# Two-layer hybrid decoder on one core: two idle token corners lent to the weight loads, adding evictions of 512 columns, and a new table of places for the wide products

## The chip, the cores and the metric

The kernel runs on 1 core of one Trainium2 chip. The metric is device microseconds of one execution; the time of a kernel is the median of several timed runs. Engines are named as in the profile: PE (TensorE), PEld (its weight loads), DVE (VectorE), ACT (ScalarE), POOL (GpSimd), SP (SyncE, here only an issuer of DMAs).

## What is computed

A causal decoder trunk of two layers over 256 tokens of width 2048, in float32:

```
for i in range(2):
    h = rms_norm(x, mix_norm_g[i])
    x = x + (fox_attention(h) if i == 0 else dilated_attention(h))
    h = rms_norm(x, mlp_norm_g[i])
    a = relu(h @ mlp_w_up[i])            # 2048 -> 8192
    x = x + (a * a) @ mlp_w_down[i]      # 8192 -> 2048
```

Layer 0 mixes with 16 heads of softmax attention with a cumulative forget-gate bias, layer 1 with three groups of dilated windows. For this change the two MLPs matter: each reads 64 MiB of `mlp_w_up` and 64 MiB of `mlp_w_down` once.

## The kernel before

**Products in three matmuls.** A weight tile is 256 rows by 512 columns (`raw`, 512 KB, two row chunks of 128). It is loaded by a DMA that SP issues (L386), cast on ACT to a rounded high part `wh` (L411), and DVE subtracts to get the low part `wl` (L412). Activations are held in the same two parts, with tokens along the stationary side. Each 128x128 by 128x512 product is three matmuls: high by high, high by low, low by high (L457 to L459). One such weight tile, used for two row chunks and two halves of the 256 tokens, is twelve matmuls; it is called a plain unit below, and the kernel counts such units (`woven["count"]`).

**The MLP in blocks.** An MLP is worked in four blocks b of 2048 inner columns: the up products of block b in four column chunks n, squared relu, and the down products of block b, whose sums are added into the residual `x`. Between them the inner activations are turned around by way of memory: DVE transposes (`turned`, L1088), POOL issues the DMAs that write `held` (L1082), SP issues the DMA that reads `back` (L367), and ACT and DVE split `back` into `aTh` (L1113) and `aTl` (L1117, L1120).

**Wide pieces.** Block 0's up products are plain units. The up products of blocks 1 to 3 are done in six wide pieces, two column chunks each, by a scheme with seven products where the plain way has eight. A piece is 8 triples and 4 single units. A triple takes two `raw` tiles (loaded crosswise) and makes three units: the first of `raw` itself, the second of differences `sd` (L408), the third of `v` (L414, L415). On DVE a triple is the op on `sd`, two of half size for `v`, and three for `wl`; on PE it is three units of six matmuls each (L1167 to L1169), into six PSUM banks. A single unit is one more `raw` tile for six matmuls. When a piece is complete, DVE combines the six banks in six ops (`c`, L1134 to L1141), ACT does relu and square (L1146, L1153, L1076), and the way around memory follows.

**Order.** All engines are fed in the order in which the program is traced; `pin` ties every engine to it. The wide units are woven between plain units by the table `WIDE_AT`: row i holds, for piece i, the counts of plain units behind which its 8 triples and its 4 single units stand (the third unit of a triple stands one count later). Counts 0 to 63 are block 0 (up, then down), 64 to 95 the down products of block 1, 96 to 127 of block 2, 128 to 159 of block 3. In blocks 2 and 3 three of the four down products are done in two halves.

**Buffers.** There are 5 `raw` tiles, 5 `wh` and 5 `wl`. When unit u has been traced on PE, the split (cast and subtract) of unit u+5 is traced behind it, and then the loads for which a `raw` tile comes free. So a split can start when PE has done the unit five places back, and DVE can be ahead of PE by up to five units. SP's loads each wait for the split that frees their tile, and SP works strictly in order: a `back` move that waits for its `held` writes holds up the loads behind it.

**Late evictions.** The down products of blocks 0 to 2, and the first halves of block 3's, are added into `x` by DMA (`late`): ACT scales the PSUM bank into a buffer `y` (L1020) and POOL issues a DMA that adds it to `x` (L1021). For each product there are four such evictions of 256 columns; the two of token half 0 use the two `bias` buffers, those of half 1 the buffers `t0` and `t2`. The next product uses the same two PSUM banks, so its first matmul waits for these evictions; the token halves are ordered so that half 0 is complete six matmuls before half 1.

**Tokens.** The normalised tokens are held as eight tiles `hT` (L566), each two chunks of 128 columns, high and low part, 256 tokens. In the wide scheme the second chunk of a pair with the second token half (the corner) is read by none of the seven products, only by block 0's plain up products.

Of the kernel before, what the change touches and what calls it, by code (L numbers as in the profile page):

```python
# [9 lines left out]
F32 = mybir.dt.float32  # L10
# [3 lines left out]
ALU = mybir.AluOpType  # L14
# [35 lines left out]
WIDE_AT = ((15, 19, 23, 27, 30, 32, 33, 34, 37, 38, 39, 39),  # L50
# [79 lines left out]
def trunk(ctx: ExitStack, tc, x, fox_w_in, fox_b_f, fox_q_gain, fox_k_gain, fox_w_out, dil_w_in,  # L130
# [244 lines left out]
    state = {"raw": 0, "split": 0, "done": 0}  # L375
    raws, splits = [], []

    def load():
# [3 lines left out]
        t = wpool.tile([P, RAW_SUB, NC], F32, tag="raw", name=f"raw{i}", bufs=RAW_BUFS)  # L382
# [67 lines left out]
    def product_steps(acc, keys, lhs, steps, post=None, begin=0, end=KC - 1):  # L450

        def three(k, t):
            hi, lo = (in_turn(w[:, k % W_SUB, :]) for w in splits[used[0]])
            ah, al = lhs(k)
            tok = slice(t * P, (t + 1) * P)
            first, last = k == begin, k == end
            nc.tensor.matmul(acc[t], ah[:, tok], hi, start=first, stop=False)  # L457
            nc.tensor.matmul(acc[t], ah[:, tok], lo, start=False, stop=False)  # L458
            nc.tensor.matmul(acc[t], al[:, tok], hi, start=False, stop=last)  # L459
# [45 lines left out]
    def last_product(keys, lhs, ready, begin):  # L505
# [7 lines left out]
        for k, x in steps:  # L513
# [4 lines left out]
            ah, al = lhs(k)  # L518
            tok = slice(t * P, (t + 1) * P)
            first, last = k == begin, k == KC - 1  # L520
            to = acc[x][:, 0:cols.stop - cols.start]
            nc.tensor.matmul(to, ah[:, tok], hi, start=first, stop=False)
            nc.tensor.matmul(to, ah[:, tok], lo, start=False, stop=False)
            nc.tensor.matmul(to, al[:, tok], hi, start=False, stop=last)
# [11 lines left out]
    def norm_begin(tag):  # L536
        rstd[tag] = small.tile([P, NT], F32, tag="rstd", name=f"rstd_{tag}", bufs=2)
        hT[tag] = [None] * (KC // 2)
        return small.tile([P, NT, NX], F32, tag="ssp", name=f"ssp_{tag}", bufs=2)

    def transposed_by_dma(tag, col, n):
# [22 lines left out]
        for half in range(2):  # L564
            pr = n * 2 + half
            both = act.tile([P, 2, 2, S], F32R, tag="hT", name=f"hT_{tag}_{pr}", bufs=KC // 2)  # L566
            if tag != "n2":
# [8 lines left out]
                of = [(both[:, i, 1, :], room[i].rearrange("p t n -> p (t n)"), both[:, i, 0, :]) for i in range(2)]  # L576
                for _, whole, hi in of:
                    nc.scalar.copy(hi, whole)
# [769 lines left out]
```

## Time and profile before

| | before |
|---|---|
| median of 3 timed runs | 2090.97 us (2090.74 to 2092.85) |
| profiled execution, its own time | 2093.61 us |
| its span | 2091.9 us |
| granted TensorE clock, mean | 0.999 |
| busy: PE, DVE, ACT, POOL | 2074.1, 1782.8, 1336.6, 319.8 us |
| HBM read and written | 488.29 MB, 40.39 MB |

The profile is of one execution. A row of the timeline gives start, duration, engine, line, operation and, in brackets, how long the engine stood idle before it and what ended that. Consecutive like instructions are merged (x4). A row of a list of waits gives who waited for whom, the total in us, the number of times and the longest. A row of a list of groups gives count, busy time, mean ns of one and the idle time before them. Matmuls are pipelined: a 512-column matmul is shown as 0.38 us long, while the next starts some 0.216 us after it.

### The profile page before, as it was taken

The page shows a single profiled execution, that of the slowest core. Times are in us where ns is not written, and L with a number is a line of the kernel's source. Part 1 is how long each engine was busy: PE and PEld are TensorE (multiplying, and loading weights), DVE is VectorE, ACT ScalarE, POOL GpSimd, SP SyncE. Part 2 cuts the span into 40 slices and gives each one's busy share as a digit, 9 for nine tenths or more (in the row PEclk, how much of TensorE's full clock was granted, in tenths as well). Part 3 has the DMA queues.
Part 4 walks back from the last instruction along what each step waited for, and adds up shares of the span by engine and source line. Part 5 has one row for each costly group of instructions (what it writes and reads, how often), then busy time and mean ns, then how long its engine had stood idle before and what let it go on. Part 6 is the DMA issues. An engine that isn't in the chain of part 4 may idle for free.

```text
span 2091.9 us, 29264 instructions
## 1 busy us (share of the span) xinstructions
PE 2074.1 (99%) x9791; PEld 1809.8 (87%) x9791; DVE 1782.8 (85%) x2267; ACT 1336.6 (64%) x1889; POOL 319.8 (15%) x446
## 2 busy tenths in 40 slices
PE   9999999999999999999999999999999999999999
PEld 7888888888888888888888888888888888888888
DVE  6788876899999999997768787767999998999985
ACT  6665654867676676775656565646767666667663
POOL 2000000113120213312010010000113031132240
PEclk9999999999999999999999999999999999999999
DMA  8888887888898999989977776867888898899896
GB/s 258 255 259 262 259 247 216 267 278 284 263 304 250 282 278 282 302 264 285 283 241 230 248 243 210 267 205 239 270 272 284 269 291 261 280 274 283 281 289 195
DMA packets 366295, 549.55 MB, mean 263 GB/s; under 512 B 44648, under 2 KB 151488, under 8 KB 366144
## 3 DMA queue, kind: packets, MB, share of 16 engines
q1 hardware_dynamic: 336800, 511.61, 76.4%
q0 software_dynamic: 28928, 35.68, 8.0%
q8 instruction: 77, 1.26, 0.2%
q14 instruction: 74, 0.61, 0.1%
q10 hardware_dynamic: 416, 0.39, 0.1%
HBM read 488.29 MB, written 40.39 MB: 253 GB/s over the span
## 4 chain that ended last, share of the span: by engine, by line
PE 76%; DVE 11%; DMA 6%; issue 4%; ACT 2%; POOL 0%; SPq 0%; DVEq 0%; ACTq 0%
PE acc L457 20%; PE acc L458 20%; PE acc L459 20%; DVE wl L412 7%; DMA raw<-in_mlp_w_up_dram 3%; DMA raw<-in_mlp_w_down_dram 2%; DVE sd L408 2%; PE wide_n_tp L1169 2%; PE wide_n_tp L1168 2%; PE wide_n_tp L1167 2%; PE wide_n_sc L1168 1%; PE wide_n_sc L1169 1%; PE wide_n_sc L1167 1%; PE wide_n_acc L1169 1%; PE wide_n_acc L1168 1%
## 5 line engine op out<-in xcount | busy, mean ns | idle before, releaser
L412 DVE TENSOR_TENSOR wl<-raw,wh 128x1024 fp32r<-128x1024 f32 (+1 forms) x755 | 910.7, 1213 | 240.9 <-ACT wh L411 232.2
L411 ACT CAST wh<-raw 128x1024 fp32r<-128x1024 f32 (+1 forms) x755 | 782.1, 1044 | 467.3 <-PE acc L459 307.1
L457 PE MATMUL acc<-wh,hT_n 128*128 128x512 f32 x1152 | 437.9, 380 | 0.2 <-ACT hT_n L653 0.2
L458 PE MATMUL acc<-wl,hT_n 128*128 128x512 f32 x1152 | 437.0, 379 | 0.5 <-DVE wl L412 0.5
L459 PE MATMUL acc<-wh,hT_n 128*128 128x512 f32 x1152 | 436.8, 379 | 0.0
L459 PEld LDWEIGHTS acc<-wh,hT_n 128*128 128x128 f32 x1152 | 217.7, 189 | 31.4 <-DVE hT_n L654 0.4
L458 PEld LDWEIGHTS acc<-wl,hT_n 128*128 128x128 f32 x1152 | 217.9, 189 | 30.8 <-DVE wl L412 1.8
L457 PEld LDWEIGHTS acc<-wh,hT_n 128*128 128x128 f32 x1152 | 217.9, 189 | 30.1 <-ACT hT_n L653 0.4
L1021 POOL DMA_DIRECT2D x<-y_n x144 | 128.8, 1242 | 524.2 <-ACT y_n L1020 522.5
L457 PE MATMUL acc<-wh,aTh_n1a 128*128 128x512 f32 x512 | 194.6, 380 | 3.7 <-ACT y_n L1020 3.7
L458 PE MATMUL acc<-wl,aTh_n1a 128*128 128x512 f32 x512 | 194.2, 379 | 0.1
L459 PE MATMUL acc<-wh,aTl_n1a 128*128 128x512 f32 x512 | 194.0, 379 | 0.0
L457 PE MATMUL acc<-wh,aTh_n3a 128*128 128x512 f32 x480 | 183.1, 382 | 3.3 <-ACT y_n L1020 3.2
L458 PE MATMUL acc<-wl,aTh_n3a 128*128 128x512 f32 x480 | 182.9, 381 | 0.2 <-DVE wl L412 0.2
L459 PE MATMUL acc<-wh,aTl_n3a 128*128 128x512 f32 x480 | 182.5, 380 | 0.0
L411 ACT CAST wh<-sd 128x1024 fp32r<-128x1024 f32 x96 | 100.7, 1049 | 116.8 <-DVE sd L408 110.7
L408 DVE TENSOR_TENSOR sd<-raw,raw 128x1024 f32<-128x1024 f32 x96 | 116.9, 1218 | 8.5 <-DMA raw<-in_mlp_w_up_dram 7.4
L411 ACT CAST wh<-v 128x1024 fp32r<-128x1024 f32 x96 | 100.9, 1051 | 36.2 <-PE acc L459 17.9
L412 DVE TENSOR_TENSOR wl<-v,wh 128x1024 fp32r<-128x1024 f32 x96 | 116.7, 1216 | 3.5 <-ACT wh L411 3.2
L412 DVE TENSOR_TENSOR wl<-sd,wh 128x1024 fp32r<-128x1024 f32 x96 | 116.6, 1215 | 0.5 <-ACT wh L411 0.4
L457 PEld LDWEIGHTS acc<-wh,aTh_n1a 128*128 128x128 f32 x512 | 96.8, 189 | 19.3 <-ACT y_n L1020 5.7
L458 PEld LDWEIGHTS acc<-wl,aTh_n1a 128*128 128x128 f32 x512 | 96.8, 189 | 14.2 <-DVE wl L412 0.6
(667 smaller groups left out, 3465.3 us busy)
## 6 DMA issues: line engine op xcount, KB each, us to landing
raw<-in_mlp_w_up_dram SPq DMA_DIRECT2D x304, 512.0 KB, 4.9
raw<-in_mlp_w_down_dram SPq DMA_DIRECT2D x256, 512.0 KB, 5.3
raw<-in_dil_w_in_dram SPq DMA_DIRECT2D x192, 256.0 KB, 3.5
raw<-in_fox_w_in_dram SPq DMA_DIRECT2D x94, 512.0 KB, 4.9
x<-y_n POOLq DMA_DIRECT2D x144, 128.0 KB, 6.6
raw<-in_fox_w_out_dram SPq DMA_DIRECT2D x32, 512.0 KB, 5.0
raw<-in_dil_w_in_dram SPq DMA_DIRECT2D x32, 512.0 KB, 4.7
raw<-in_dil_w_out_dram SPq DMA_DIRECT2D x32, 512.0 KB, 3.7
```

The costliest lines, as they stand in the source:

```text
L408: nc.vector.tensor_sub(quarters[0], raw, raws[n - 1][:, 1, :].unsqueeze(1).to_broadcast([P, RAW_SUB, NC]))
L411: nc.scalar.copy(hi[:, part, :], raw[:, part, :])
L412: nc.vector.tensor_sub(lo[:, part, :], raw[:, part, :], hi[:, part, :].bitcast(F32))
L457: nc.tensor.matmul(acc[t], ah[:, tok], hi, start=first, stop=False)
L458: nc.tensor.matmul(acc[t], ah[:, tok], lo, start=False, stop=False)
L459: nc.tensor.matmul(acc[t], al[:, tok], hi, start=False, stop=last)
L1021: nc.gpsimd.dma_start(xt[n][:, t, h * HC:h * HC + HC], y, accum_op=ALU.add)
L1167: nc.tensor.matmul(banks[bank], ah, wh, start=what < 3 and of == 0, stop=False, **alone)
L1168: nc.tensor.matmul(banks[bank], ah, wl, start=False, stop=False, **alone)
L1169: nc.tensor.matmul(banks[bank], al, wh, start=False, stop=of == KC // 2 - 1, **alone)
```

## The change

1. **Tokens in three tiles.** Each norm now puts its tokens into one large tile `hT` and two smaller ones with tag `hc`, reached by `tokens_of`. For the MLP norms (n1, n3) the two `hc` tiles hold the corners, four pairs each; for n0 and n2 they hold the last two pairs. In the MLP norms the second chunk of a pair is now split in two ops of 128 columns on ACT and two on DVE, where one of 256 stood.
2. **Two more raw tiles.** An `hc` tile is as large as a `raw` tile. From the end of block 0's up products until the down products of block 3 begin (`corners["free"]`), loads may go into the two `hc` tiles too, so that 7 weight tiles are loaded or held instead of 5. Each of the two sets is refilled as its oldest tile is used up.
3. **Adding evictions of 512 columns.** Per token half one eviction and one adding DMA of 512 columns, both halves in the `bias` buffers, instead of two of 256.
4. **The table `WIDE_AT`**: most triples and single units stand 1 or 2 counts earlier.
5. Side effects of 1: the gate product of layer 0 reads high and low parts interleaved; its small tiles share one tile `gates`.

```
 WIDE_AT = ((16, 19, 23, 27, 30, 32, 33, 35, 37, 38, 39, 39),      # was 15, 19, 23, 27, 30, 32, 33, 34, 37, 38, 39, 39
            (41, 43, 45, 47, 49, 51, 53, 56, 58, 58, 58, 60),      # was 42, 44, 47, 49, 51, 52, 55, 56, 58, 58, 60, 61
...
            (117, 119, 120, 122, 124, 126, 127, 129, 131, 131, 131, 131))  # was 118, 120, 122, 123, 125, 126, 127, 128, 131, 131, 132, 132
...
+    pooled, corners = [0], {"free": False, "users": []}
...
-        t = wpool.tile([P, RAW_SUB, NC], F32, tag="raw", name=f"raw{i}", bufs=RAW_BUFS)
+        if corners["free"] and len(corners["users"]) < 2:
+            t = act.tile([P, RAW_SUB, NC], F32, tag="hc", name=f"raw{i}", bufs=2)
+            corners["users"].append(i)
+        else:
+            t = wpool.tile([P, RAW_SUB, NC], F32, tag="raw", name=f"raw{i}", bufs=RAW_BUFS)
+            pooled.append(i)
...
-        while state["done"] in spent:
-            state["done"] += 1
-        while state["raw"] < min(len(plan), state["done"] + RAW_BUFS):
+        while state["raw"] < len(plan):
+            for users in (pooled, corners["users"]):
+                while users and users[0] in spent:
+                    users.pop(0)
+            if len(pooled) >= RAW_BUFS and not (corners["free"] and len(corners["users"]) < 2):
+                break
             load()
...
-                of = [(both[:, i, 1, :], room[i].rearrange("p t n -> p (t n)"), both[:, i, 0, :]) for i in range(2)]
+                of = [(tokens(pr, 0, 1), room[0], tokens(pr, 0, 0))]
+                of += [(tokens(pr, 1, 1, t), room[1][:, t], tokens(pr, 1, 0, t)) for t in range(NT)]
...
+            hT[tag].append(act.tile([P, KC // 2 * 6 * P], F32R, tag="hT", name=f"hT_{tag}"))
+            hT[tag] += [act.tile([P, 8 * P], F32R, tag="hc", name=f"hc_{tag}_{n}", bufs=2) for n in range(2)]
...
             if late:
-                for h in range(2):
-                    of, bufs = ("bias", 2) if t == 0 else (("t0", "t2")[h], 1)
-                    y = work.tile([P, HC], F32, tag=of, name=f"y_{scale}_{n}_{t}_{h}_{used[0]}", bufs=bufs)
-                    nc.scalar.activation(y, by_column(acc[t])[:, 0, h, :], AF.Copy, scale=rstd[scale, 2][:, t:t + 1])
-                    nc.gpsimd.dma_start(xt[n][:, t, h * HC:h * HC + HC], y, accum_op=ALU.add)
+                y = work.tile([P, NC], F32, tag="bias", name=f"y_{scale}_{n}_{t}_{used[0]}", bufs=2)
+                nc.scalar.activation(halves(y), by_column(acc[t]), AF.Copy, scale=rstd[scale, 2][:, t:t + 1])
+                nc.gpsimd.dma_start(xt[n][:, t, :], y, accum_op=ALU.add)
...
+            corners["free"] = b < 3
```

How the table moves instructions is shown at two places of the first MLP. The first is on DVE, at the last two triples of its last wide piece (in the table's last row, counts 127 and 128 before, 127 and 129 now). A triple is the row that writes `sd`, the row for `wl` from `raw` behind it, two rows for `v`, and the rows for `wl` from `sd` and from `v`; a row for `wl` from `raw` elsewhere is a plain unit. Before:

```order
1017 L412 TENSOR_TENSOR wl_8917<-raw_8827,wh_8916 128x1024
1018 L412 TENSOR_TENSOR wl_8935<-v_8890,wh_8934 128x1024
1019 L408 TENSOR_TENSOR sd_8946<-raw_8860,raw_8829 128x1024
1020 L412 TENSOR_TENSOR wl_8945<-raw_8860,wh_8944 128x1024
1021 L414 TENSOR_TENSOR v_8947<-raw_8860,sd_8946 128x512
1022 L415 TENSOR_TENSOR v_8947<-raw_8829,v_8947 128x512
1023 L412 TENSOR_TENSOR wl_8964<-sd_8946,wh_8963 128x1024
1024 L412 TENSOR_TENSOR wl_8974<-raw_8896,wh_8973 128x1024
1025 L412 TENSOR_TENSOR wl_9004<-v_8947,wh_9003 128x1024
1026 L408 TENSOR_TENSOR sd_9015<-raw_8920,raw_8898 128x1024
1027 L412 TENSOR_TENSOR wl_9014<-raw_8920,wh_9013 128x1024
```

The same place of DVE now:

```order
1027 L418 TENSOR_TENSOR wl_8837<-raw_8702,wh_8836 128x1024
1028 L418 TENSOR_TENSOR wl_8849<-v_8798,wh_8848 128x1024
1029 L414 TENSOR_TENSOR sd_8866<-raw_8726,raw_8724 128x1024
1030 L418 TENSOR_TENSOR wl_8865<-raw_8726,wh_8864 128x1024
1031 L420 TENSOR_TENSOR v_8867<-raw_8726,sd_8866 128x512
1032 L421 TENSOR_TENSOR v_8867<-raw_8724,v_8867 128x512
1033 L418 TENSOR_TENSOR wl_8884<-sd_8866,wh_8883 128x1024
1034 L418 TENSOR_TENSOR wl_8894<-raw_8759,wh_8893 128x1024
1035 L418 TENSOR_TENSOR wl_8918<-v_8867,wh_8917 128x1024
1036 L418 TENSOR_TENSOR wl_8928<-raw_8787,wh_8927 128x1024
1037 L414 TENSOR_TENSOR sd_8941<-raw_8806,raw_8804 128x1024
1038 L418 TENSOR_TENSOR wl_8940<-raw_8806,wh_8939 128x1024
```

Between one triple and the next there was one plain unit (1024); now there are two (1034, 1036).

The second place is on ACT, at the end of block 0's last down product, where its sums are evicted and block 1 begins (`c` are tiles of the wide piece that has just been completed). Before:

```order
541 L411 CAST wh_6063<-raw_5979 128x1024
542 L1113 CAST aTh_n1a_0_6054<-back_n1a_0_1_5965 128x4x128
543 L1153 ACTIVATE c_n1a_2_3_6086<-wide_n_1_2_tp_5303 128x512
544 L411 CAST wh_6088<-sd_6065 128x1024
545 L1146 ACTIVATE c_n1a_2_1_5915<-c_n1a_2_1_5915 128x512
546 L1076 ACTIVATE c_n1a_2_3_6086<-c_n1a_2_3_6086 128x512
547 L1076 ACTIVATE c_n1a_2_1_5915<-c_n1a_2_1_5915 128x512
548 L411 CAST wh_6110<-raw_6002 128x1024
549 L1020 ACTIVATE y_n_3_0_0_247_6122<-acc_0_5832,rstd_n_4109 128x256
550 L1020 ACTIVATE y_n_3_0_1_247_6125<-acc_0_5832,rstd_n_4109 128x256
551 L1020 ACTIVATE y_n_3_1_0_247_6137<-acc_1_5833,rstd_n_4109 128x256
552 L1020 ACTIVATE y_n_3_1_1_247_6140<-acc_1_5833,rstd_n_4109 128x256
```

Now:

```order
545 L417 CAST wh_6042<-raw_5930 128x1024
546 L1133 CAST aTh_n1a_0_6055<-back_n1a_0_0_5932 128x4x128
547 L1166 ACTIVATE c_n1a_2_1_5901<-c_n1a_2_1_5901 128x512
548 L1133 CAST aTh_n1a_0_6055<-back_n1a_0_1_5948 128x4x128
549 L1096 ACTIVATE c_n1a_2_3_6040<-c_n1a_2_3_6040 128x512
550 L1096 ACTIVATE c_n1a_2_1_5901<-c_n1a_2_1_5901 128x512
551 L417 CAST wh_6077<-sd_6044 128x1024
552 L417 CAST wh_6099<-raw_5946 128x1024
553 L1040 ACTIVATE y_n_3_0_247_6118<-acc_0_5828,rstd_n_4109 128x512
554 L1040 ACTIVATE y_n_3_1_247_6131<-acc_1_5829,rstd_n_4109 128x512
```

Two evictions stand where four stood, and the relu (L1153 before) has moved ahead of these rows; the casts, the squares and one more cast of `back` still stand between the first cast and the evictions.

More of the change, by code (lines that the diff above doesn't have):

```diff
@@ L453, in three @@
             hi, lo = (in_turn(w[:, k % W_SUB, :]) for w in splits[used[0]])
-            ah, al = lhs(k)
-            tok = slice(t * P, (t + 1) * P)
+            ah, al = (x[t] for x in lhs(k))
             first, last = k == begin, k == end
-            nc.tensor.matmul(acc[t], ah[:, tok], hi, start=first, stop=False)
-            nc.tensor.matmul(acc[t], ah[:, tok], lo, start=False, stop=False)
-            nc.tensor.matmul(acc[t], al[:, tok], hi, start=False, stop=last)
+            nc.tensor.matmul(acc[t], ah, hi, start=first, stop=False)
+            nc.tensor.matmul(acc[t], ah, lo, start=False, stop=False)
+            nc.tensor.matmul(acc[t], al, hi, start=False, stop=last)
         for k in steps[::W_SUB]:
@@ L565, in transposed_by_dma @@
             pr = n * 2 + half
-            both = act.tile([P, 2, 2, S], F32R, tag="hT", name=f"hT_{tag}_{pr}", bufs=KC // 2)
+            tokens = tokens_of(tag)
             if tag != "n2":
@@ L675, in norm_chain, with blocks @@
             jobs.done.add((tag, "rstd"))
+    def blocks(x):
+        return [x[:, t * P:(t + 1) * P] for t in range(NT)]
     def lhs_h(tag):
         def get(k):
-            both = hT[tag][k // 2]
-            return both[:, k % 2, 0, :], both[:, k % 2, 1, :]
+            return [[tokens_of(tag)(k // 2, k % 2, x, t) for t in range(NT)] for x in range(2)]
         return get
@@ L851, in gate_chain @@
             nc.tensor.transpose(pft[:, t, :], f[:, t * P:(t + 1) * P], ident[:2 * FH, :2 * FH])
-        z = small.tile([P, NT, FH], F32, tag="g_z", name="g_z", bufs=1)
+        z, neg, e, u, u2, s, lf = (gates[:, i] for i in range(7))
         for t in range(NT):
@@ L1219, in mlp @@
             out_proj(chunks,
-                     lambda k, b=b, aT=aT: tuple(x[:, k % 4, :] for x in aT[place(b, k) // 4]),
+                     lambda k, b=b, aT=aT: [blocks(x[:, k % 4, :]) for x in aT[place(b, k) // 4]],
                      scale=tag, group=3 if b == 3 else 0, parts=LAST_DOWN_PARTS, halved=HALVED[b],
@@ L1307, in trunk @@
     out_proj(lambda n: lambda k: ("of", k),
[L1308 removed]
+             lambda k: [blocks(x[:, k % 4, :]) for x in oT["f", k // 4]],
              normed("n1", MLP_G), group=3)
```

65 lines of the change are left out of this document (35 added, 30 removed), and 10 rows, old and new, of the table WIDE_AT.

## The prediction

> **What bounds the kernel now.** The page comes first: PE is busy in all but 17.8 of 2091.9 us.
>
> ```profile
> PE 2074.1 (99%) x9791; PEld 1809.8 (87%) x9791; DVE 1782.8 (85%) x2267; ACT 1336.6 (64%) x1889; POOL 319.8 (15%) x446
> ```
>
> So the change can only win back time in which PE stands. The list of PE's waits says for whom (total us, times, longest):
>
> ```profile
> PE acc L457 <- ACT y_n L1020: 6.9, 7, 1.9
> PE wide_n_sc L1168 <- DVE wl L412: 4.6, 9, 0.9
> PE acc L458 <- DVE wl L412: 0.7, 3, 0.3
> ```
>
> 19 stalls, 12.2 us, nearly all in the two MLPs: seven because an eviction `y` of the PSUM bank is late, twelve because the low part of a weight tile is. What one costs is more than its bracket, as PE's timeline at the longest of the first MLP shows:
>
> ```profile
> 604.77 0.38 PE L457 MATMUL acc<-wh,aTh_n1a 128*128 128x512 f32 x1
> ...
> 605.20 0.38 PE L459 MATMUL acc<-wh,aTl_n1a 128*128 128x512 f32 x1
> 607.36 0.48 PE L457 MATMUL acc<-wh,aTh_n1a 128*128 128x512 f32 x1 [1.78 <-ACT y_n L1020]
> 607.68 0.38 PE L458 MATMUL acc<-wl,aTh_n1a 128*128 128x512 f32 x1
> ```
>
> Undisturbed starts are 0.215 us apart (0.43 for two). Here the start is 2.16 later, then 0.32: 2.05 lost in all, the bracket plus 0.26. With 0.26 on each, the 19 cost 12.2 + 4.9 = 17.1 us. That, and what follows from it, is the most to be had.
>
> Why was `y` late? ACT's timeline just before:
>
> ```profile
> 601.07 1.05 ACT L411 CAST wh<-raw 128x1024 fp32r<-128x1024 f32 x1 [2.95 <-DMA raw<-in_mlp_w_up_dram]
> ...
> 605.54 1.03 ACT L411 CAST wh<-raw 128x1024 fp32r<-128x1024 f32 x1
> 606.48 1.56 ACT L1020 ACTIVATE y_n<-acc,rstd_n 128x256 f32<-128x256 f32 x4
> ```
>
> ACT lost 2.95 us to a weight tile that had not landed, and the eviction, which PE needed at 605.4, queued behind the casts. The root is a late load. The second MLP has it worse:
>
> ```profile
> 1881.09 1.05 ACT L411 CAST wh<-raw 128x1024 fp32r<-128x1024 f32 x1 [3.13 <-DMA raw<-in_mlp_w_up_dram]
> ...
> 1886.45 1.05 ACT L411 CAST wh<-raw 128x1024 fp32r<-128x1024 f32 x1 [2.08 <-DMA raw<-in_mlp_w_down_dram]
> ```
>
> Here SP's rows show what held the loads: two `back` moves, the second ending 4.99 us after the first began, and only then the next load; the list of SP's waits says that such moves wait for `held`.
>
> ```profile
> 1876.18 4.99 SPq L367 DMA_DIRECT2D back_n3a<-held_n3a  x2
> 1881.27 0.38 SPq L386 DMA_DIRECT2D raw<-in_mlp_w_down_dram  x1
> ```
>
> ```profile
> SPq L367 <- DMA held_n3a<-turned_n3a: 39.6, 24, 4.2
> ```
>
> PE pays for it with 1.90 + 0.26, and more: the clock drops.
>
> ```profile
> 1889.24 0.48 PE L457 MATMUL acc<-wh,aTh_n3a 128*128 128x512 f32 x1 [1.90 <-ACT y_n L1020]
> ...
> 1889.99 0.57 PE L457 MATMUL acc<-wh,aTh_n3a 128*128 128x512 f32 x1
> ...
> 1893.62 0.38 PE L1167 MATMUL wide_n_acc<-wh,sums_n 128*128 128x512 f32 x1
> ```
>
> ```profile
> 1890.00:1900.00 10.00, 10.00 (x40) 8.47 (x39) 9.65 (x10) 5.91 (x6) 2.64 (x3) 0.83 1.04 286
> ```
>
> The granted clock (third from the end) is 0.83 in this window; nine steps take 3.63 us where nine of 0.215 take 1.94: another 1.7 us.
>
> The twelve stalls on `wl` have another root: DVE's throughput. One triple and one plain unit on DVE, in its timeline:
>
> ```profile
> 906.35 1.22 DVE L408 TENSOR_TENSOR sd<-raw,raw 128x1024 f32<-128x1024 f32 x1
> ...
> 909.35 0.69 DVE L415 TENSOR_TENSOR v<-raw,v 128x512 f32<-128x512 f32 x1
> 909.95 1.22 DVE L412 TENSOR_TENSOR wl<-sd,wh 128x1024 fp32r<-128x1024 f32 x1
> 911.09 1.22 DVE L412 TENSOR_TENSOR wl<-raw,wh 128x1024 fp32r<-128x1024 f32 x1
> ...
> 913.36 1.22 DVE L408 TENSOR_TENSOR sd<-raw,raw 128x1024 f32<-128x1024 f32 x1
> ```
>
> From `sd` to `sd` 7.01 us without a pause (1.14 per op of 1024 columns, 0.60 of 512). PE needs 30 matmuls of 0.215 for these four units, 6.45. Triples at every count let PE gain 0.56 on DVE each time, until it stands; a plain unit without a triple (DVE 1.14, PE 2.58) gives back 1.44. The loads are not the limit there: DVE 9.93 of 10 us busy, DMA at 0.49.
>
> ```profile
> 900.00:910.00 10.00, 9.51 (x45) 8.01 (x44) 9.93 (x12) 6.32 (x8) 0.00 (x0) 1.00 0.49 166
> ```
>
> **The change part by part**, against the profiled execution's own 2093.6.
>
> A. *Seven raw tiles where a late load caused the stall.* The loads stand two tiles earlier before their use, that is by two units of PE time, 2.6 us at the least (two of six matmuls) and 5.2 for plain ones. That covers most waits of 2 to 3 us as quoted; what holds SP still stands. Three places: 2.05 at 607, 2.16 and 1.7 at 1889, and the first row here, 0.82 + 0.26:
>
> ```profile
> 1684.08 0.48 PE L457 MATMUL acc<-wh,aTh_n3a 128*128 128x512 f32 x1 [0.82 <-ACT y_n L1020]
> 945.83 0.48 PE L457 MATMUL acc<-wh,aTh_n1a 128*128 128x512 f32 x1 [1.32 <-ACT y_n L1020]
> 2025.22 0.48 PE L457 MATMUL acc<-wh,aTh_n3a 128*128 128x512 f32 x1 [0.48 <-ACT y_n L1020]
> ```
>
> Together 7.0. The casts and squares stay ahead of the evictions, so some 0.6 may stay at each: I take -5.2, bounds 0 and -7.0.
>
> The clock is weighed by itself. The row: a stall of 1.9 us, and 0.83 behind it. The Trainium skill ("TensorE: Matmul & The Clock Gate", section "Part 1: The HAM clock gate (the "warmup" mystery)") lets the clock fall to half only after an idle window of about 3.4 us; by it this stall was too short, the drop has another cause, and removing the stall returns 1.7 less. The trace speaks against the rule as a strict bound, since the slow steps follow right behind the stall, and for its length, 3.6 us.
>
> B. *The two other rows*, 1.58 and 0.74. They fall into block 3's down products, where the corners take no new loads; only what was loaded ahead helps. Half: -1.1, bounds 0 and -2.3.
>
> C. *The table.* The stalls on `wl`:
>
> ```profile
> 796.54 0.48 PE L1168 MATMUL wide_n_sc<-wl,sums_n 128*128 128x512 f32 x1 [0.89 <-DVE wl L412]
> 904.22 0.48 PE L1168 MATMUL wide_n_sc<-wl,sums_n 128*128 128x512 f32 x1 [0.49 <-DVE wl L412]
> 911.23 0.48 PE L1168 MATMUL wide_n_sc<-wl,sums_n 128*128 128x512 f32 x1 [0.26 <-DVE wl L412]
> 918.23 0.48 PE L1168 MATMUL wide_n_sc<-wl,sums_n 128*128 128x512 f32 x1 [0.26 <-DVE wl L412]
> 1873.77 0.48 PE L1168 MATMUL wide_n_sc<-wl,sums_n 128*128 128x512 f32 x1 [0.91 <-DVE wl L412]
> ```
>
> The three near 910 are the last four triples of the last piece, at counts 125 to 128. From the first `sd` to the fourth `wl` of differences DVE has 18 ops of 1024 and 10 of 512, 18 x 1.14 + 10 x 0.60 = 26.5; PE up to there 3 plain units and 10 of six matmuls, 96 x 0.215 = 20.6: DVE falls back by 5.9. Now they stand at 124, 126, 127, 129: 20 and 12 ops, 30.0, against 5 and 10 units, 25.8: 4.2. That is 1.7 less, about all that was lost there (1.0 + 3 x 0.26 = 1.8), in each MLP: -3.4. The stalls at 796 and 1873 stand at the first triples of the fifth piece, where DVE also combines the fourth: before 17 ops of 1024 and 16 of 512 against 4 plain units and 9 others, 29.0 to 21.9; now 18 and 16 against 5 and 9, 30.1 to 24.5. 1.5 less, of which I take 0.8 in each MLP, since the next triples are as dense as before: -1.6. C is -5.0, bounds -8 (all twelve gone) and +2 (the earlier triples fill places that had slack).
>
> D. *Evictions of 512.* The groups of ACT bound it:
>
> ```profile
> L1020 ACT ACTIVATE y_n<-acc,rstd_n 128x256 f32<-128x256 f32 x144 | 58.4, 470 | 18.1 <-PE acc L459 11.8 <-DMA x<-y_n 5.7
> L1068 ACT ACTIVATE a_n1a<-acc 128x512 f32<-128x512 f32 x8 | 4.3, 593 | 0.0
> ```
>
> Four in 1.56 us (row at 606.48) become two of some 0.59: the bank is free 0.2 to 0.3 us earlier after 36 products. Of the seven stalls two are left (6.9 less the five quoted, 0.6 us): there it counts, -0.6; elsewhere it is slack. In the new order on ACT two evictions in each MLP stand right behind a cast of `sd`, where before two others did, so that sort of stall stays. The transfers double:
>
> ```profile
> x<-y_n POOLq DMA_DIRECT2D x144, 128.0 KB, 6.6
> ```
>
> Landing is then between 6.6 and 13.2 us; the buffer is wanted again a product later, at least four plain units or 10.3 us. I take the lower, it costs nothing; at the upper a half product waits 3 us, which the other pair of PSUM banks covers.
>
> E. *Norms.* 32 casts on ACT like this one, and as many subtractions, half of which become two of 128 columns:
>
> ```profile
> L578 ACT CAST hT_n<-room_n 128x256 fp32r<-128x256 f32 x32 | 11.1, 394 | 0.0
> ```
>
> 16 more casts, 0 to 6.3 us of ACT, at a place where PE stalls on `wl` now (the third row of its waits): +0.6.
>
> Sum: -5.2 - 1.1 - 5.0 - 0.6 + 0.6 = -11.3, so 2082.3 on the profiled execution. That one lies 2.6 above the median; the drop of the clock, 1.7 of it, need not be in the timed runs, so I count 9.6 against 2091.0: **2081.4**. What is late next is ACT's queue ahead of the evictions in block 3.
>
> **The rivals.**
>
> *DVE alone is the bound.* More loads in hand then only mean that tiles wait for DVE, and evictions still queue behind casts that wait for `sd`. For it: DMA at 0.49 at 900. Against it: the rows at 601 and 1881, where ACT waits for DMA. Only C and D count, -5.6 and +0.6, and with half of C gone to new dense places some -4: 2087.
>
> *Stalls change places.* All six rows of the table move; each hole closed can open another, at a `y` behind an `sd` or where `back` lands. A to E cancel: 2091.
>
> *The deeper load queue holds up `back`* (slower). `back` goes by the same queue as the weights. Two more loads ahead of it are 1.05 MB, 3.7 us at the 286 GB/s of the window at 1890. ACT waits for it already:
>
> ```profile
> ACT aTh_n3a L1113 <- DMA back_n3a<-held_n3a: 15.0, 10, 3.0
> ```
>
> Ten times, so 20 in both MLPs (an estimate); each 3.7 later, of which a plain unit of cover takes 2.6: 20 x 1.1 = +22, against C's -5: 2108. It decides if the two loads are still under way when `back` is issued. Against it: a load is issued only when a tile is used up, so the two extra ones have landed long before. The Trainium skill ("DMA: Bandwidth & Descriptors", section "Queues, rings and completion order") says that each DMA engine takes a ring's descriptors in order, which is this rival's mechanism; no run here shows it yet.
>
> **How the numbers follow.** About 0.2% (4.2 us) is what a measurement of this kernel tells from no change. Forecast 0.66 (faster); DVE alone 0.16, half of it faster and half within; places 0.11 (within); `back` 0.07 (slower). So faster 0.74, same 0.19, slower 0.07. The range goes from 2077 (A and C near their bounds) to 2091: it leaves out `back`, and some 0.1 of the ends.
>
> **What would show it.** Right: ACT's waits for `raw` mostly gone, no drop of the clock at 1890, PE's stalls near 607, 910, 1684, 1889 and 1990 gone, those of block 3 and one near 800 left. A is wrong if ACT still waits 2 us and more for `raw` in blocks 1 and 2; C, if `wl` stalls of the same sum stand elsewhere; the whole, if ACT's waits for `back` have grown.

## The result and the profile after

| | before | after |
|---|---|---|
| median of 6 timed runs each, same chip | 2092.06 us (2090.74 to 2094.46) | 2076.99 us (2075.56 to 2078.86) |
| profiled execution, its own time | 2093.61 us | 2075.86 us |
| its span | 2091.9 us | 2074.1 us |

The ratio after to before is 0.9926, with a 95% interval of 0.9913 to 0.9939: 15.1 us faster. The forecast, 2081.4, had the direction, and the mechanism in part. It was 4.4 us too slow, and its range ended at 2077.0, just above the median. One execution among all runs below, of e15, took 3101.5 us at a granted clock of 0.66; the median of e15 leaves it out.

The first part of the page after, busy time, share and instructions of each engine:

```profile
PE 2067.7 (100%) x9791; PEld 1809.4 (87%) x9791; DVE 1780.5 (86%) x2283; ACT 1328.0 (64%) x1833; POOL 253.7 (12%) x374
```

PE stood 17.8 us of its span before and stands 6.4 now. The list of PE's waits after (total us, times, longest):

```profile
PE spare L185 <- DVE zeros L181: 1.1, 1, 1.1
PE acc L466 <- DVE wl L418: 1.1, 4, 0.6
PE acc L465 <- ACT hT_n L678: 0.2, 1, 0.2
```

No row has `y_n` any more, and none a wide product. What is left of `wl` is four stalls, the longest of them in the norm phase at 382 us. At the place of the first long stall PE's timeline after has two steps of 0.25 and 0.32 us instead of 0.215, 0.14 late in all, and no bracket:

```profile
604.97 0.38 PE L467 MATMUL acc<-wh,aTl_n1a 128*128 128x512 f32 x1
605.22 0.48 PE L465 MATMUL acc<-wh,aTh_n1a 128*128 128x512 f32 x1
605.54 0.38 PE L466 MATMUL acc<-wl,aTh_n1a 128*128 128x512 f32 x1
```

ACT's waits after, of which the prediction spoke:

```profile
ACT wh L417 <- DVE sd L414: 131.3, 80, 3.0
...
ACT aTh_n3a L1133 <- DMA back_n3a<-held_n3a: 13.0, 10, 2.3
ACT aTh_n1a L1133 <- DMA back_n1a<-held_n1a: 11.4, 8, 2.9
...
ACT wh L417 <- DMA raw<-in_mlp_w_up_dram: 8.5, 10, 2.1
ACT wh L417 <- DMA raw<-in_mlp_w_down_dram: 7.8, 7, 2.4
```

The MLP loads are waited for 16.3 us in sum, where before they were waited for 85.3. SP's list shows that this is not because SP stands less before the `back` moves:

```profile
SPq L367 <- DMA held_n3a<-turned_n3a: 46.3, 26, 5.7
```

That row was 39.6 us before. SP stands as long as ever; two loads more are simply in hand meanwhile. Where ACT still waits agrees with this. The corners are lent from the first down product of block 0 to the first of block 3, in the kernel after from 469 to 907 us and from 1539 to 1976 on PE. ACT's brackets for the MLP's `raw` within these stretches sum to 2.2 us (71.5 before), the longest 1.02; the other 14.0 (13.8 before) stand outside, where both kernels load into five tiles.

The groups for the new evictions and their transfers (count, busy us, mean ns, idle before):

```profile
L1040 ACT ACTIVATE y_n<-acc,rstd_n 128x512 f32<-128x512 f32 x72 | 47.5, 683 | 15.1 <-PE acc L467 8.4 <-DMA x<-y_n 6.1
L1041 POOL DMA_DIRECT2D x<-y_n x72 | 63.7, 956 | 648.1 <-ACT y_n L1040 645.6 <-ACT aTh_n3a L1133 1.0 <-DMA held_n1a<-turned_n1a 0.5
```

### The profile page after: what moved, and what is told of

It is laid out like the page before. It is cut to its first block, busy times and chain, and to the rows that moved or that the text cites. A ratio compares the mean times of both kernels' runs of the same rounds, so it can differ in the third digit from the quotient of the medians.

```text
span 2074.1 us, 28993 instructions
## 1 busy us (share of the span) xinstructions
PE 2067.7 (100%) x9791; PEld 1809.4 (87%) x9791; DVE 1780.5 (86%) x2283; ACT 1328.0 (64%) x1833; POOL 253.7 (12%) x374
## 4 chain that ended last, share of the span: by engine, by line
PE 86%; issue 6%; DVE 4%; DMA 1%; ACT 1%; POOL 1%; SPq 0%; DVEq 0%; ACTq 0%; POOLq 0%
PE acc L466 22%; PE acc L467 22%; PE acc L465 22%; PE wide_n_tp L1187 2%; PE wide_n_tp L1188 2%; PE wide_n_tp L1189 2%; DVE wl L418 2%; PE wide_n_sc L1188 2%; PE wide_n_acc L1187 2%; PE wide_n_sc L1187 2%; PE wide_n_sc L1189 2%; PE wide_n_acc L1188 2%; PE wide_n_acc L1189 2%; DMA x<-y_n 1%; ACT wh L417 1%
## 5 line engine op out<-in xcount | busy, mean ns | idle before, releaser
L465 PE MATMUL acc<-wh,hT_n 128*128 128x512 f32 x864 | 328.7, 380 | 0.2 <-ACT hT_n L678 0.2
L466 PE MATMUL acc<-wl,hT_n 128*128 128x512 f32 x864 | 327.8, 379 | 0.9 <-DVE wl L418 0.8
L467 PE MATMUL acc<-wh,hT_n 128*128 128x512 f32 x864 | 327.7, 379 | 0.0
L466 PEld LDWEIGHTS acc<-wl,hT_n 128*128 128x128 f32 x864 | 163.4, 189 | 23.9 <-DVE wl L418 2.0
L467 PEld LDWEIGHTS acc<-wh,hT_n 128*128 128x128 f32 x864 | 163.3, 189 | 23.7 <-DVE hT_n L679 0.4
L465 PEld LDWEIGHTS acc<-wh,hT_n 128*128 128x128 f32 x864 | 163.4, 189 | 23.1 <-ACT hT_n L586 0.8
L1041 POOL DMA_DIRECT2D x<-y_n x72 | 63.7, 956 | 648.1 <-ACT y_n L1040 645.6
L465 PE MATMUL acc<-wh,hc_n 128*128 128x512 f32 x288 | 109.3, 380 | 0.0
```

The source lines that it names most:

```text
L465: nc.tensor.matmul(acc[t], ah, hi, start=first, stop=False)
L466: nc.tensor.matmul(acc[t], ah, lo, start=False, stop=False)
L467: nc.tensor.matmul(acc[t], al, hi, start=False, stop=last)
L1041: nc.gpsimd.dma_start(xt[n][:, t, :], y, accum_op=ALU.add)
```

## The theories, and a table of all runs

The trace says that the stalls are gone, not which edit took them. These theories were set against each other:

- **1, late loads.** The raw tiles take the stalls on `y`, the table those on `wl`; each can be had without the other. This is how the forecast added its terms.
- **2, DVE alone.** The density of the triples makes everything late: the table does nearly all, the tiles nearly nothing.
- **3, one lead.** Tiles and table feed one and the same lead of the splits over PE: either edit alone removes much of both kinds of stall.
- **4, POOL.** Half the issues free POOL, `held` and `back` come earlier, and so the loads.

Two further theories, 5a and 5b, came from the first results and are told where they were tried. The columns of the table: edits in force (T two more raw tiles, W new table, E new evictions; all but e3, e11, e12 and e16 have the new token layout), median against the median of the kernel before in the same batch (2092.1 to 2094.0), the ratio's 95% interval, and from the lists of waits the sums of PE's waits for `y`, for `wl`, and of ACT's waits for the MLP's `raw`.

| run | edits | us | interval | PE: y | PE: wl | ACT: raw |
|---|---|---|---|---|---|---|
| before | none | 0 | | 6.9 | 5.3 | 85.3 |
| e1 | layout alone | +0.6 | 0.9992 to 1.0010 | 5.4 | 6.8 | 86.9 |
| e2 | T | -5.1 | 0.9967 to 0.9987 | 2.2 | 4.3 | 12.8 |
| e3 | W alone | +9.7 | 1.0026 to 1.0052 | 9.1 | 8.4 | 110.0 |
| e4 | E | +1.6 | 0.9997 to 1.0014 | 5.5 | 8.7 | 91.8 |
| e5 | W, E | +6.8 | 1.0022 to 1.0049 | 3.9 | 9.0 | 108.7 |
| e6 | T, E | -7.0 | 0.9956 to 0.9981 | 0.2 | 5.5 | 8.6 |
| e7 | T, W | -15.4 | 0.9919 to 0.9944 | 0.2 | 1.6 | 15.8 |
| e8 | one tile, W, E | -9.6 | 0.9941 to 0.9968 | 0 | 5.0 | 30.3 |
| after | T, W, E | -15.1 | 0.9913 to 0.9939 | 0 | 1.1 | 16.3 |

## Experiments: the parts by themselves

**e1, the new layout alone.** The kernel after with

```
-            corners["free"] = b < 3
+            corners["free"] = False
```

and the old table and evictions. 

> The kernel after with three of its four parts taken back: the corners are never lent to the loads (5 raw tiles), the old table, the old evictions of 256 columns. What is left is the new layout of the tokens, with split casts in the MLP norms. All theories: +0.3 to +0.8 us against the kernel before (the forecast's term E is +0.6), with PE's stalls on the evictions y and on wl standing where they stood.

Measured +0.6, which the interval cannot tell from nothing; its stalls stand where they stood. The layout is no part of the gain.

**e2, the tiles.** The kernel after with the old table and the old evictions. 

> Layout and the two more raw tiles; old table, old evictions. Theory 1, late loads, in full: the stalls on y go altogether, the clock's drop too, 7.0 + 2.3 us of places A and B, less 0.6 for the layout: -8.7 against the kernel before, and the stalls on wl (4.6 + 0.26 x 9 = 6.9 us) stay. The forecast as it stood: -5.2 - 1.1 + 0.6 = -5.7. Theory 2, DVE's throughput is the bound: 0 to -1, y still late behind casts that wait for sd. Theory 3, both run down one and the same lead of five units, so that either edit alone removes much of both kinds of stall: -11 or more, with stalls on wl gone as well.

Measured -5.1 (the forecast's -5.7, not theory 1's -8.7 nor theory 3's -11; theory 2 falls). Its lists of waits, PE first and then ACT:

```profile
PE wide_n_sc L1191 <- DVE wl L418: 4.1, 10, 0.9
PE acc L465 <- ACT y_n L1043: 2.2, 6, 0.6
```

```profile
ACT wh L417 <- DMA raw<-in_mlp_w_up_dram: 7.4, 8, 2.5
...
ACT wh L417 <- DMA raw<-in_mlp_w_down_dram: 5.4, 10, 1.2
```

The late loads are gone (within the lent stretches ACT waits for none) and the long stalls with them; of `y` six stalls of 0.3 to 0.6 are left, and most of the stalls on `wl` (4.3 of 5.3 us).

**e3, the table.** The kernel before with the new `WIDE_AT`. 

> The kernel before with the new table alone. Theory 1: the stalls on wl go, -5 to -7, those on y stay about where ACT waits for raw. Theory 2: -11 to -14, since the density of triples is what makes everything late. Theory 3: -8 to -11, stalls of both kinds shrink. Rival of the forecast, stalls change places: within 2 us of the kernel before.

Measured +9.7: none of the theories. Its lists of waits, PE and ACT:

```profile
PE acc L457 <- ACT y_n L1020: 9.1, 10, 1.6
PE wide_n_sc L1168 <- DVE wl L412: 6.6, 8, 2.1
```

```profile
ACT wh L411 <- DMA raw<-in_mlp_w_up_dram: 91.6, 62, 4.4
...
ACT wh L411 <- DMA raw<-in_mlp_w_down_dram: 18.4, 23, 2.4
```

With five tiles the new table makes loads later, and with them both kinds of stall longer.

**e4, the evictions.** The kernel after with `corners["free"] = False` and the old table. 

> Layout and the evictions of 512 columns; 5 raw tiles, old table. All theories of the loads and of DVE: +0.6 for the layout less 0.6 for the evictions, 0 in sum (-1 to +0.6). Theory 4, POOL freed by half its issues lets the moves by memory and so the loads start earlier: -4 or more, with SP's wait for held shorter than 39.6 us in sum.

Measured +1.6, which the interval does not tell from nothing; SP's wait for `held` (n3a) is 33.4 us, shorter than 39.6, and nothing is gained by it. Theory 4 falls.

## Experiments: each part taken out of the kernel after

**e5, without the tiles** (`corners["free"] = False`). 

> The kernel after without the two more raw tiles: new table, new evictions, layout. Against the kernel before: theory 1, late loads, -5 to -7 (the late evictions of A and B are back, some 9 us above the kernel after). Theory 2, DVE's throughput: -13 to -15, since the table does it. Theory 3, one lead for both: -9 to -12, some 4 us above the kernel after.

Measured +6.8 against the kernel before, 22 us above the kernel after: far outside what any theory had. One place shows how. SP's timeline:

```profile
788.82 6.15 SPq L367 DMA_DIRECT2D back_n1a<-held_n1a  x2
795.08 1.04 SPq L392 DMA_DIRECT2D raw<-in_mlp_w_up_dram  x2
796.23 0.88 SPq L392 DMA_DIRECT2D raw<-in_mlp_w_down_dram  x1
798.02 1.50 SPq L392 DMA_DIRECT2D raw<-in_mlp_w_up_dram  x2
```

ACT's and DVE's:

```profile
803.19 1.05 ACT L417 CAST wh<-raw 128x1024 fp32r<-128x1024 f32 x1 [5.49 <-DMA raw<-in_mlp_w_up_dram]
```

```profile
803.22 1.23 DVE L414 TENSOR_TENSOR sd<-raw,raw 128x1024 f32<-128x1024 f32 x1 [4.08 <-DMA raw<-in_mlp_w_up_dram]
```

PE's:

```profile
805.63 0.48 PE L1188 MATMUL wide_n_tp<-wl,hT_n 128*128 128x512 f32 x1 [0.85 <-DVE wl L418]
...
809.30 0.48 PE L1188 MATMUL wide_n_sc<-wl,sums_n 128*128 128x512 f32 x1 [2.11 <-DVE wl L418]
```

The loads come in a burst behind the `back` moves: five of 512 KB issued from 795.08 on, 2.62 MB, which the window's 305 GB/s carries in 8.6 us (row below: us, busy times, clock, DMA share, GB/s). DVE, the busiest engine but PE, does 3.92 us of work in 8.

```profile
796.00:804.00 8.00, 8.00 (x39) 6.92 (x37) 3.92 (x4) 2.51 (x4) 0.00 (x0) 1.00 1.02 305
```

In the kernel after SP stands just as long at that place, and DVE works through. Rows of SP, then the window after:

```profile
786.19 6.43 SPq L367 DMA_DIRECT2D back_n1a<-held_n1a  x2
792.73 0.63 SPq L392 DMA_DIRECT2D raw<-in_mlp_w_down_dram  x1
793.46 2.02 SPq L392 DMA_DIRECT2D raw<-in_mlp_w_up_dram  x2
```

```profile
793.00:801.00 8.00, 8.00 (x39) 7.00 (x38) 7.97 (x10) 4.75 (x6) 0.00 (x0) 1.00 1.01 278
```

So a stall on `wl`, which the forecast gave to DVE's throughput, can have a late load as its root too.

**e6, with the old table.** 

> The kernel after with the old table: 7 raw tiles, new evictions, layout. Against the kernel before: theory 1, -8 to -10, the stalls on wl at 796, 904 to 918 and 1873 are there. Theory 2: 0 to -2. Theory 3: -11 to -13, stalls on wl smaller than before, since sd and v no longer start late.

Measured -7.0; PE's list shows what is lost against the kernel after:

```profile
PE wide_n_sc L1188 <- DVE wl L418: 4.7, 10, 0.9
...
PE acc L465 <- ACT y_n L1040: 0.2, 1, 0.2
```

With the tiles in, the table is worth 2085.56 - 2076.99 = 8.6 us (8.0 when each is taken against the kernel before in its own batch). Against e2, the rest of the `y` stalls is gone (2.2 to 0.2); the 1.9 us between the two times are within the intervals.

**e7, with the old evictions.** 

> The kernel after with the old evictions of 256 columns in four buffers: 7 raw tiles, new table. Theories 1 to 3: -14 to -15, 0 to 1 us above the kernel after, since with nothing late ahead of them the evictions have slack. Theory 4, POOL's issues matter: -10 or less, and SP's wait for held longer than in the kernel after (46.3 us for n3a).

Measured -15.4, the same as the kernel after: once table and tiles are in, nothing is left for the evictions to take.

**e8, one corner instead of two** (`len(corners["users"]) < 1`). 

> The kernel after with one corner lent instead of two: 6 raw tiles. Theory 1: a load stands one unit of PE time earlier, 1.3 to 2.6 us, which covers half of the waits of 2 to 3 us: about halfway between the kernel without lent corners and the kernel after. Theory 2: as the kernel after, within 1 us. Theory 3: within 1 to 2 us above the kernel after.

Measured -9.6. From five tiles to six to seven (e5, e8, after) ACT's waits for `raw` go 108.7, 30.3, 16.3 us and the medians 2099.4, 2083.0, 2077.0: the sixth tile brings 16.4, the seventh 6.0. Not halfway, as theory 1 had it: most comes with the first tile. Within the lent stretches alone the waits go 94.5, 16.1, 2.2.

Theory 1 so has the tiles right and the table wrong: without the tiles it gains nothing. Theory 3 falls as it was set, since neither edit alone takes much of both kinds of stall (e2, e3).

## Experiments: why the table needs the tiles

Two causes were open for the late loads of e3 and e5: SP standing before the `back` moves (5a), or too few tiles for the time that a load takes (5b). **e9** is e5, and **e10** the kernel after, with

```
-            move(back[t], held[t].rearrange("j c i x -> (j c) (i x)"))
+            nc.gpsimd.dma_start(back[t], held[t].rearrange("j c i x -> (j c) (i x)"))
```

so that SP carries loads alone. 

> The kernel with the new table, layout and evictions but 5 raw tiles (its median was 6.8 us above the kernel before), with one more edit: POOL issues the `back` moves, so that SP carries loads alone and never stands before them. Theory 5a, SP standing at `back` makes the loads late: most of ACT's 108.7 us of waits for raw goes and the time falls by 10 us or more, towards the kernel after. Theory 5b, five tiles are too few for a load of 5 us: ACT's waits for raw stay above 70 us and the time falls by less than 5 us. Against both: if the y transfers or held now wait behind back on POOL, the time grows.

> The kernel after with the same edit: POOL issues the `back` moves. With seven tiles SP's standing (46.3 and 40.6 us of waits for held) is covered by the loads in hand: 5a and 5b both give no gain, within 1 us of the kernel after. Slower by 2 us or more, if back comes later on POOL's queue behind the adding transfers.

Measured: e9 +28.8 against the kernel before (ratio 1.0137, interval 1.0123 to 1.0151), e10 +12.7 (1.0066, 1.0050 to 1.0081). ACT's waits in e9:

```profile
ACT wh L417 <- DMA raw<-in_mlp_w_up_dram: 86.0, 68, 7.0
ACT aTh_n1a L1133 <- DMA back_n1a<-held_n1a: 26.7, 12, 4.8
ACT aTh_n3a L1133 <- DMA back_n3a<-held_n3a: 26.4, 11, 5.2
ACT wh L417 <- DMA raw<-in_mlp_w_down_dram: 17.6, 13, 5.3
```

Two things follow. With SP free of `back` the MLP's loads are still waited for 103.6 us (108.7 in e5), and within the lent stretches 94.5 (94.5 in e5); in e10, with the same edit and seven tiles, it is 0.3 there, so it is not the edit that makes them late. Standing before `back` is not what makes most of them late, and 5a falls as the main cause. SP's own list in e9 shows what it waits for instead, tiles that DVE has not used up:

```profile
SPq L392 <- DVE wl L418: 836.4, 447, 6.3
SPq L392 <- DVE v L420: 297.1, 96, 7.2
```

In e5 these were 742.0 and 258.3 (in e10, where the loads are in time, 844.0 and 238.8, so these sums alone do not tell a late load). And `back` comes later on POOL's queue (waits of 53.1 us in e9 against 13.0 in e5), which PE feels: in both runs there are two stalls of 2.1 us on `aTl`, and with those on `aTh` they make 7.4 of the 15.6 us by which PE's stalls grew from e5 to e9. So the time grew for another reason and says nothing for 5b by itself; the waits for `raw` and the row of e8 do.

**e11, the last row of the table alone, and e12, the fifth alone,** both in the kernel before. 

> The kernel before with only the last row of the new table (the sixth piece). The forecast's ledger of DVE's work: -3.4 us, the stalls on wl at 904, 911, 918 and 1985, 1992, 1999 gone. Theory 5b: the triples now stand a count earlier at places where loads are short, so that ACT's waits for raw grow and the gain is given back there: -1 to +2.

> The kernel before with only the fifth row of the new table (counts 102, 103, 104, 107 ... become 101, 102, 103, 106 ...). The forecast's ledger: -1.6 us. Theory 5b: new stalls of about 2 us on wl near 812 and 1895, where the kernel with the whole new table and five tiles has them, so +2 to +5, with the clock's drop there as well if a stall passes 1.9 us.

Measured +0.3 (0.9989 to 1.0008) and +1.6 (0.9999 to 1.0017). In e11 one of the six stalls that the forecast wanted gone is left (0.42 at 1992). In their place PE waits 0.35 for `wl` at 878 and at 1956, and evictions come later: 1.63 at 811 and 1.06 at 1910, where the kernel before has no bracket. The 2-us stalls that 5b wanted in e12 are not there either: a stall on `wl` of 1.9 us or more stands only in e3, e5 and e8, all with the whole new table and fewer than seven tiles.

Then each row was taken back in the kernel after: **e13** the last, **e14** the fifth, **e15** rows 1 to 4; and **e16** put the new rows 1 to 4 alone into the kernel before. 

> The kernel after with the last row of the old table. If the ledger sizes it once loads are in hand: +3.4 us above the kernel after, with stalls on wl near 904, 911, 918 and 1985, 1992, 1999 back. If the row is worth nothing, as by itself in the kernel before: within 1 us of the kernel after.

> The kernel after with the fifth row of the old table. The forecast's share of the ledger: +1.6 us above the kernel after (half of the 1.5 in each MLP). The stalls of the kernel with the old table and seven tiles (1.05 and 0.45 at 797 and 815, 1.06 and 0.92 at 1870 and 1889, each with 0.1 behind it) less what is left there in the kernel after: about +3.

> The kernel after with rows 1 to 4 of the old table. The forecast left these rows at nothing: within 1 us of the kernel after. If they hold part of the table's gain: the rest of 8.6 after e13 and e14, some +2.

> The kernel before with rows 1 to 4 of the new table alone (five tiles). If the table's loss with five tiles lies in these rows: +7 to +9 above the kernel before, with new stalls near 631, 647, 707 and 722. If it comes of the rows together, one piece running late into the next: +1 to +3.

Measured, medians against the kernel after (2076.99, another batch): e13 +0.3, e14 +4.4, e15 +7.2. Against the kernel before in their own batch they are -16.7, -12.7 and -9.8, where the kernel after had -15.1, so the first three numbers are good to some 2 us only. e16 against the kernel before: +4.3 (1.0014 to 1.0032). Of the stalls of the last four triples, which have the same counts in e13 as before, one is left in the first MLP, PE's timeline:

```profile
905.27 0.38 PE L1188 MATMUL wide_n_sc<-wl,sums_n 128*128 128x512 f32 x1
...
912.13 0.48 PE L1188 MATMUL wide_n_sc<-wl,sums_n 128*128 128x512 f32 x1 [0.23 <-DVE wl L418]
```

The same triples with the same ledger stalled 0.49, 0.26 and 0.26 before, and 0.31, 0.27 and 0.26 in e6, which has seven tiles as well. What differs between e6 and e13 are the rows ahead of the last: in e13 the fifth piece ends at count 115 and the sixth begins at 118, in e6 and before it is 117 and 118. What decides is the lead with which DVE comes into a piece, and the timelines show it: the time from the end of DVE's `wl` of differences to PE's first matmul that reads it (us), at the first, fourth and eighth triple of the sixth piece in the first MLP. At 0.05 or 0.06 PE starts as soon as the tile is there.

| | first | fourth | eighth |
|---|---|---|---|
| before | 2.25 | 1.54 | 0.06 |
| e6 | 2.43 | 1.59 | 0.05 |
| e13 | 3.54 | 2.75 | 0.05 |
| after | 2.10 | 2.23 | 2.08 |

With the old row the lead runs down to nothing: before and in e6 from the sixth triple on, in e13, which comes in with 1.1 us more, only at the last. With the new row it holds. So old and new row differ in lead, but with e13's head start the old one costs PE next to nothing. That the lead at the start comes from the distance between the end of one piece and the start of the next fits these runs, but is argued. This distance is 1 count before and 2 after at the last two seams (101 to 102 and 117 to 118; 99 to 101 and 115 to 117). Where a mixture of rows makes it 0 (e11, e12, e14, e15), PE waits in addition for ACT's `c`, as in e15's list; of the kernels with a distance of 1 or more only e9, with its late `back`, has such a row:

```profile
PE wide_n_sc L1188 <- DVE wl L418: 3.6, 4, 0.9
...
PE wide_n_tp L1187 <- ACT c_n1a L1173: 0.3, 1, 0.3
PE wide_n_tp L1187 <- ACT c_n3a L1173: 0.3, 1, 0.3
```

So e14 and e15 hold seams that neither kernel has, and their times are not shares of the gain. Whether the rows add the runs do not tell: e13 to e15 sum to 11.9, or to 6.0 by their own batch, where the whole table is worth 8.6 or 8.0. With five tiles it is 0.3 + 1.6 + 4.3 = 6.2 by parts and 9.7 together, a difference within the intervals.

## Why the prediction was right or wrong, point by point

**The bound: right.** 17.1 us in 19 stalls, and 1.7 of the clock, was the most to be had on the profiled execution; its own time fell by 17.75.

**The step that failed is the sum**, -5.2 - 1.1 - 5.0 - 0.6 + 0.6: each term was priced as if its edit stood alone, and then they were added. By themselves the edits give -5.7 (tiles, e2 against e1), +9.7 (table, e3) and +1.1 (evictions, e4 against e1), in sum near +5; together they give -15. By place, on the two profiled executions and with 0.26 us on each stall as the prediction counted it, every term that forecast a gain came out larger: A 7.0 for 5.2, B 2.3 for 1.1, C 6.3 for 5.0 (the twelve stalls on `wl`, 8.4, less the four that are left, 2.1), and the two other stalls on `y` 1.1 for D's 0.6. That is 16.7 of the 17.75, where the terms had 11.9. What the forecast held back (0.6 at each place of A, half of B) was not needed, because the other edits take what one edit leaves. That C came near its size is luck: its working counted on the table by itself, which costs time.

**A, -5.2: mis-sized; 7.0 measured in place.** The cause, a late load, was right, and so was what it held back ("some 0.6 may stay at each"), for the tiles alone: e2 has brackets of 0.30, 0.30 and 0.40 at 606, 1680 and 1883, with 0.26 each 0.6 in the mean. But the new evictions (e6) or the table (e7) take these leftovers: `y` is waited for 0.2 us in either. The rows at 607, 1684 and 1889 are gone.

**The clock, 1.7, was left out of the median**, since it need not be in the timed runs. That was right: of the 71 timed executions of the kernel before in the later batches 62 have a mean granted clock of 1.0, and nine have the 0.999 of the profiled one. On the profiled execution the drop went with the stall: from 1880 to 1900 us the kernel after has a clock of 1.00. The median itself was taken from three runs, 2091.0; six gave 2092.1. The two profiled executions lie 17.75 apart, the medians 15.1: 1.55 of the difference is how far the profiled execution of before lay above its median, 1.13 how far that of after lay below its own.

**B, -1.1: mis-sized; 2.3 measured in place.** The reason, no new loads in block 3's corners, was no limit: neither place has a bracket left. Tiles alone leave 0.61 at 942 (e2).

**C, -5.0: wrong in its working.** The ledger of DVE against PE gave -3.4 to the last row and -1.6 to the fifth. e11 and e12 measured +0.3 and +1.6, and the whole table without tiles +9.7, outside the bound of +2; behind the tiles it is -8.6. Behind them the last row by itself is worth 0.3 (e13), not 3.4. Two things were missing in the ledger. It began with the first triple of a piece, as if DVE came to it with the same lead in every kernel; e13 shows the same ledger with one stall of 0.23 in the first MLP and one of 0.22 in the second, where the kernel before has three in each. And it took the loads at 900 for no limit ("DVE 9.93 of 10 us busy, DMA at 0.49"), which held for that window and not for those near 800, where with the new table DVE worked 3.92 of 8 us.

**D, -0.6: not told apart from nothing (0.3 between e7 and the kernel after, 1.9 between e2 and e6, both within the intervals), and wrong in a price.** An eviction of 512 columns from the down product takes 683 ns, not 590; nothing waits for it. The transfers land in 7.0 us, near the end that was taken:

```profile
x<-y_n POOLq DMA_DIRECT2D x72, 256.0 KB, 7.0
```

**E, +0.6:** e1 gave +0.6, and cannot tell it from nothing.

**The rivals.** DVE alone falls with e2, e3 and e6; its price was also added up wrongly, since -5.6 and +0.6 with half of C gone make -2.5, not -4. Stalls change places is what happened wherever the table stood without the tiles or a row without its neighbours, not in the whole change. The deeper queue holds up `back` falls: ACT's waits for it fell from 27.8 to 24.4 us in sum, and where they did grow with seven tiles (37.5 in e2, 33.7 in e13) PE did not feel it. The ring order of the Trainium skill ("DMA: Bandwidth & Descriptors", section "Queues, rings and completion order") was named as that rival's mechanism; no run here shows it either way.

**The signs named beforehand** were right but for what was to be left: the stalls of block 3 are gone too, and near 800 only one of 0.18 stands. The sign against A, waits of 2 us and more for `raw` in blocks 1 and 2, did not come: ACT's three waits of that size, 2.13, 2.19 and 2.38 at 1474, 960 and 2031, stand in block 0's up products and block 3's down products, outside the lent stretches, and the longest in blocks 1 and 2 is 1.02.

## What to carry to other kernels

Edits that feed the same reserve, here the splits' lead over the matmuls, have no prices of their own: a denser schedule costs 10 us without the buffers that it draws on and brings 8 to 9 with them, so they have to be tried as a set, and a part that measures slower by itself is not for that reason a bad part. A ledger of two engines' work over a stretch needs the lead at its start as much as the difference within it; and an engine that shows as busy in one window can be starved in another, so the window of the stall itself has to be read. A stall behind the engine that seems to be the bound is worth following one step further back, to the load.

## What the runs showed of the hardware

**Half rate behind a stall.** Six single stalls of 1.90 to 2.11 us (before, e3, e5 twice, e8, e9) were each followed, 0.4 to 1.3 us after their end, by a stretch at a granted clock of 0.50, with matmuls that start 0.43 us apart instead of 0.215. One in e9, of 2.01, was not. None of the 22 single stalls of 1.40 to 1.84 us was. (Four pairs of stalls within 3 us, in e9 and e10, were followed by such a stretch as well.) Each stretch lasts 3.41 us, two of those behind pairs twice that, and costs half of it, 1.7 us.

What decides is not the stall's length but how much of it falls into one window. Within each run the stretches begin whole multiples of 3.413 us apart: in e5 at 809.67 and 1891.70, which is 317 of them, in e9 at 967.02, 1895.44 and 2059.28, which is 272 and 48. So the trace shows a clock that is set window by window, on a grid that runs on through the kernel. Rows of such windows, first the one with e5's first stall and the one behind it, then the same for the stall of 2.01 in e9 (us, busy times with PE first; clock third from the end):

```profile
806.26:809.67 3.41, 1.30 (x7) 0.82 (x6) 3.41 (x5) 2.39 (x3) 0.00 (x0) 1.00 0.70 179
809.67:813.08 3.41, 3.41 (x10) 2.66 (x9) 3.41 (x4) 0.32 (x1) 0.00 (x0) 0.50 0.73 253
```

```profile
1868.13:1871.55 3.42, 1.72 (x8) 1.53 (x9) 3.27 (x3) 3.10 (x5) 0.85 (x1) 1.00 0.97 311
1871.55:1874.96 3.41, 3.41 (x18) 2.98 (x17) 3.38 (x6) 3.41 (x7) 0.93 (x2) 1.00 1.06 255
```

In e5 all 2.11 us lie in one window. In e9 the stall lies across two, 0.31 and 1.69 us, and the clock stays; so does that of 1.84 in e4, 0.56 and 1.29. Over all windows of the 18 traces, behind the start of the kernel, every one in which PE stood 1.90 us or more was followed by half rate, and none in which it stood 1.79 us or less was, except two that were at half rate already (1.39 and 1.65). The boundary lies between 1.79 and 1.90 us, a little over half a window.

In the Trainium skill ("TensorE: Matmul & The Clock Gate", section "Part 1: The HAM clock gate (the "warmup" mystery)") it takes an idle window of about 3.4 us; here a window that is idle for 1.90 of 3.41 is enough. The same section lets full rate come back after a busy window of about 3.4 us, and with that the 3.41 us at half rate agree. It also calls the window free-running, and the grid agrees with that.
